# Tokens transposed by a matmul with a diagonal of 1/rms, the prompt's pieces in a bank of their own, in one core's hybrid retention and RG-LRU step

## The chip, the core and the metric

The kernel runs on one core of a Trainium2 chip. Its engines work side by side, each through its own queue in program order: TensorE (PE, with its weight loads PEld), VectorE (DVE), ScalarE (ACT), GpSimd (POOL) and SyncE (SP), which here issues the DMA transfers. The metric is the device time of one execution in microseconds; a lower one is better. A measurement of three runs spreads by about 0.1%, so a difference under 0.2% counts as none.

## The reference, cut to what matters

One layer over 512 sample tokens and 128 prompt tokens of 1024 channels, all in fp32. Each group has its own shift and scale, made from a conditioning vector; the normalized and modulated tokens `h` feed one wide projection, and everything after it hangs on `h`:

```python
mod = jax.nn.silu(cond) @ w_ada + b_ada
shift, scale, gate = jnp.split(mod, 3, axis=-1)
h = rmsnorm(x, norm_w) * (1.0 + scale[:, None]) + shift[:, None]
z = h @ w_in                      # q, k, v, gates, RG-LRU inputs, merge gates
...                               # retention, RG-LRU, merge, w_out
return x + gate[:, None] * out, s_ret, s_lru
```

## The kernel before

Nearly all of the time is matmuls in three passes of fp32r parts (high x high, high x low, low x high). These are issued by `mm3` (lines 414 to 416), and the rest of the program keeps TensorE supplied. The change lies wholly in the start, before the first projection can run; there the order of each engine's work is written out by hand, and a planner (`Plan`) orders ACT and DVE only from the loop over `kt` (line 903) on. The start runs like this:

- `load_x` brings five tiles of 128 tokens (four of the sample, one of the prompt), `load_ada` and `load_wf` bring the weights of the modulation and of the first projection, all through SP's queue. Before them SP issues `pv`, a table of small vectors.
- `warm(n)` issues n matmuls of the identity with itself, 128x128 in fp32; their result is never read. It is called as `warm(8)`, then `warm(9)` after each token tile, and twice `warm(2)` between transposes. An fp32 matmul shows as two records in the trace, a transpose as one.
- `norm_x(t)`: ACT squares and sums a token tile and takes the root of the mean; DVE takes the reciprocal and scales the tile, 128x1024, in place.
- `x_T(kt)`: five transposes on TensorE, one for each token tile, bring 128 channels by 640 tokens into a PSUM tile `z` of two banks (512 sample columns in the one, 128 prompt columns in the other), and ACT or DVE copies both parts into `fulls[kt]`. There are eight `kt`, and three PSUM tiles `z` that take turns.
- `mod_mm(kt)`: eight fp32 matmuls make shift and scale of 128 channels; ACT or DVE copies them out; `mod_cols(kt)` turns them into columns by four small fp32 matmuls (lines 766 and 767), and DVE finishes `mB` and `mA`.
- `h_mod(kt)`: ACT and DVE make the modulated tokens and split them into `hTh` and `hTl`.
- `z_first(i, kt)`: six fp32r matmuls of the first projection, for three blocks i. In the loop over `kt` they alternate with `mod_mm(kt + 2)`, `mod_cols(kt + 2)`, and the splits of the weights, `wf_high` and `wf_low`.

Of the kernel before, what the change touches and what calls it, by code (L numbers as in the profile page):

```python
# [10 lines left out]
AF = mybir.ActivationFunctionType  # L11
ALU = mybir.AluOpType
MUL, ADD, SUB = ALU.mult, ALU.add, ALU.subtract
# [289 lines left out]
def tile_hybrid_step(  # L303
# [14 lines left out]
    nc = tc.nc  # L318
    S = Plan()
    act, dve, pool, pe = nc.scalar, nc.vector, nc.gpsimd, nc.tensor  # L320
    act0, dve0 = Direct(act, S, "act"), Direct(dve, S, "dve")
# [12 lines left out]
    W6, WL = Slots(S), Slots(S)  # L334
    raws.add(perm, [f"raw{i}" for i in range(4)])

    def f32(ap):
        return ap.bitcast(F32)

    def wide(name, r=False):  # L340
        return W6.take([128, NT], F32R if r else F32, name)
# [41 lines left out]


    pv = cst.tile([128, NV], F32, name="pv")
    nc.sync.dma_start(out=pv, in_=vec)
    ident = cst.tile([128, 128], F32, name="ident")
    small = cst.tile([128, 160], F32, name="small")
    sp = cst.tile([128, 28], F32, name="sp")
# [233 lines left out]
    xt = [xp.tile([128, D], F32, name=f"x{t}") for t in range(5)]  # L623
# [9 lines left out]
    def load_x(t):  # L633
        src = x_sample[128 * t:128 * t + 128, :] if t < 4 else x_prompt
        nc.sync.dma_start(out=xt[t], in_=src)

    def load_ada(kt):
        ts = []
        for c in range(4):
            t = ada.take([128, 512], F32, "adr")  # L640
            nc.sync.dma_start(out=t, in_=w_ada[kt, :, c])
            ts.append(t)
        ada_raw[kt] = ts

    def load_wf(kt):
        t = raws.take([128, 384], F32, "wfr")
        nc.sync.dma_start(out=t, in_=w_first[kt])
        wf_raw[kt] = t

    def wf_high(kt):  # L650
        wf_hl[kt] = slab.take((perm,))
        act0.activation(wf_hl[kt][0][:, 0:384], wf_raw[kt], AF.Copy)

    def wf_low(kt):
        hi, lo = wf_hl[kt]
        dve0.tensor_tensor(lo[:, 0:384], wf_raw[kt], f32(hi[:, 0:384]), op=SUB)
        raws.give(wf_raw.pop(kt))

    for t in range(5):
        load_x(t)  # L660
    for kt in range(4):
        load_ada(kt)
# [66 lines left out]
    def psz():  # L729
        return zp.tile([128, 2, 512], F32, tag="z", name="z")  # L730
# [3 lines left out]
    def warm(n):  # L734
        for _ in range(n):
            pe.matmul(out=mb[1][:, 384:512], lhsT=ident, rhs=ident, start=True, stop=True)  # L736

    warm(8)

    def norm_x(t):  # L740
        r = rst[:, t:t + 1]
        act0.activation(sq.rearrange("p a b -> p (a b)"), xt[t], AF.Square, accum_out=ssq[:, t:t + 1])
        act0.activation(r, ssq[:, t:t + 1], AF.Sqrt, scale=1.0 / D, bias=epsc)
        dve0.reciprocal(r, r)
        dve0.tensor_scalar(xt[t], xt[t], r, None, op0=MUL)

    def mod_mm(kt, eng=act0):
        b = mb[kt % 2]  # L750
        for k in range(8):
            g = slice(32 * (k % 4), 32 * (k % 4) + 32)
            w = ada_raw[kt][k // 2][:, 256 * (k % 2):256 * (k % 2) + 256]
            pe.matmul(out=b[g, 0:256], lhsT=c32[:, k], rhs=w, start=(k < 4), stop=(k > 3))
        S.pe += 1070.0
        for t in ada_raw.pop(kt):
            ada.give(t)
        if eng is act0:
            act0.activation(mod4[kt % 2], b[:, 0:256], AF.Copy)
        else:  # L760
            dve0.tensor_copy(mod4[kt % 2], b[:, 0:256])

    def mod_cols(kt):
        m, b = mod4[kt % 2], mb[kt % 2]
        sel = pv[:, V_SEL:V_SEL + 2]
        pe.matmul(out=b[:, 256:258], lhsT=m[:, 0:128], rhs=sel, start=True, stop=True)
        pe.matmul(out=b[:, 258:260], lhsT=m[:, 128:256], rhs=sel, start=True, stop=True)
        S.pe += 300.0
        dve0.tensor_scalar(mB[:, kt], b[:, 256:258], col(V_BSH, kt), None, op0=ADD)
        dve0.tensor_scalar(mA[:, kt], b[:, 258:260], bsc1[:, kt:kt + 1], col(V_NW, kt), op0=ADD, op1=MUL)  # L770

    fulls, ready = {}, {}
    groups = ((slice(0, 512), 1), (slice(512, 640), 0))

    def x_T(kt, eng=act0):
        full = wide("hf")
        fulls[kt] = full
        z = psz()
        for t in range(5):
            o = z[:, 1, 0:128] if t == 4 else z[:, 0, 128 * t:128 * t + 128]  # L780
            pe.transpose(o, xt[t][:, 128 * kt:128 * kt + 128], ident)  # L781
        for c, src in ((groups[0][0], z[:, 0]), (groups[1][0], z[:, 1, 0:128])):
            if eng is act0:
                act0.activation(full[:, c], src, AF.Copy)
            else:
                dve0.tensor_copy(full[:, c], src)

    def h_mod(kt, both=False):
        full = fulls[kt]
        for c, g in groups:  # L790
            a, b = mA[:, kt, g:g + 1], mB[:, kt, g:g + 1]
            if both:
                act0.activation(hTh[:, kt, c], full[:, c], AF.Identity, scale=a, bias=b)
        for c, g in groups:
            a, b = mA[:, kt, g:g + 1], mB[:, kt, g:g + 1]
            if both:
                dve0.tensor_scalar(full[:, c], full[:, c], a, b, op0=MUL, op1=ADD)
            else:
                act0.activation(full[:, c], full[:, c], AF.Identity, scale=a, bias=b)
        if not both:  # L800
            act0.activation(hTh[:, kt], full, AF.Copy)
        dve0.tensor_tensor(hTl[:, kt], full, f32(hTh[:, kt]), op=SUB)
        ready[kt] = S.clock["dve"]
# [58 lines left out]

    for t in range(5):
        norm_x(t)
        warm(9)
    x_T(0)
    x_T(1, dve0)
    wf_high(0)
    wf_low(0)
    warm(2)  # L870
    mod_mm(0, dve0)
    load_ada(4)
    load_wf(4)
    x_T(2)
    warm(2)
    mod_cols(0)
    x_T(3, dve0)
    x_T(4)
    h_mod(0, True)
    x_T(5)  # L880
    mod_mm(1)
    x_T(6)
    wf_high(1)
    wf_low(1)
    x_T(7)
    xtp.__exit__(None, None, None)
    ttp, tr = open_pool("ttp", "right")
    tts.add(tr, [f"tt{i}" for i in range(3)])
# [406 lines left out]
    qk, v, o, pt, kd = {}, {}, {}, {}, {}  # L1295
# [696 lines left out]
```

## Time and profile before

| | |
|---|---|
| median of three runs | 999.16 us (998.46 to 999.55) |
| the profiled execution | 999.01 us |
| its span, first to last instruction | 997.2 us |
| TensorE busy | 981.6 us, 98% of the span |
| VectorE, ScalarE busy | 732.3 us, 543.6 us |
| mean granted TensorE clock | 0.997 of full speed |

The median includes what lies outside the span, about 1.8 us in the profiled execution. Busy time of TensorE counts the warming matmuls too, so it doesn't tell useful work from filler.

### The profile page before, as it was taken

Reading aid. Unit: us, or ns where it says so; the run is one execution under the profiler, and the core shown is the slowest. Engines: PE = TensorE matmul, PEld = TensorE weight load, DVE = VectorE, ACT = ScalarE, POOL = GpSimd, SP = SyncE. Lnnn points to the kernel's source line nnn. Section 1 sums busy time; section 2 is a strip of 40 time slices with the busy share of each in tenths; the row PEclk is TensorE's granted clock in tenths of the full one; section 3 lists DMA queues with packets and bytes.
Section 4 is the critical chain, followed back from the end, with each engine's and each line's share of the span. In section 5 each row is a group of like instructions: output and inputs, shape, how many; then the busy total and the mean of one; then the engine's idle time right before and its main releaser. Section 6 shows DMA issues by size and latency. Waiting matters only on the chain.

```text
span 997.2 us, 15542 instructions
## 1 busy us (share of the span) xinstructions
PE 981.6 (98%) x6079; PEld 918.0 (92%) x6079; DVE 732.3 (73%) x1133; ACT 543.6 (55%) x856; POOL 2.2 (0%) x13
## 2 busy tenths in 40 slices
PE   9999999999999999999999999999899999999997
PEld 8889999999999999999888888888789999999886
DVE  4699977779986799783775887877768877646554
ACT  6665554486544765652468596485574535324222
POOL 0000000000000000000000000000000000000000
PEclk9999999999999999999999999999999999999999
DMA  9745444333553335344532635454627554745312
GB/s 328 247 138 171 156 142 138 127 126 131 182 172 128 111 130 178 134 138 164 190 116 101 203 116 176 136 175 153 206 93 290 191 184 165 240 124 176 118 64 84
DMA packets 62167, 158.15 MB, mean 159 GB/s; under 512 B 6906, under 2 KB 10126, under 8 KB 62094
## 3 DMA queue, kind: packets, MB, share of 16 engines
q1 hardware_dynamic: 62094, 157.16, 46.9%
q8 instruction: 47, 0.77, 0.3%
q14 instruction: 26, 0.21, 0.1%
HBM read 119.51 MB, written 37.63 MB: 158 GB/s over the span
## 4 chain that ended last, share of the span: by engine, by line
PE 91%; DVE 4%; ACT 3%; issue 1%; DMA 1%; POOL 0%; DVEq 0%; POOLq 0%; ACTq 0%
PE z L414 29%; PE z L415 29%; PE z L416 29%; PE b L736 1%; PE z L1522 1%; ACT hf L294 1%; DVE sl L420 1%; ACT hTh L294 1%; DVE hTl L294 1%; DMA y<-sg 0%; DMA yf<-y 0%; ACT sh L539 0%; PE z L781 0%; ACT gt L1181 0%; DVE st L1416 0%
## 5 line engine op out<-in xcount | busy, mean ns | idle before, releaser
L420 DVE TENSOR_TENSOR sl<-raw,sh 128x1024 fp32r<-128x1024 f32 (+1 forms) x128 | 133.2, 1045 | 50.2 <-ACT sh L505 49.8
L505 ACT ACTIVATE sh<-raw 128x1024 fp32r<-128x1024 f32 (+1 forms) x96 | 96.8, 1013 | 120.2 <-PE z L415 75.9
L414 PE MATMUL z<-sh,sh 128*128 128x320 f32 x512 | 158.5, 310 | 0.7 <-ACT p L1007 0.7
L416 PE MATMUL z<-sh,sl 128*128 128x320 f32 x512 | 158.4, 309 | 0.0
L415 PE MATMUL z<-sl,sh 128*128 128x320 f32 x512 | 158.4, 309 | 0.0
L414 PE MATMUL z<-hTh,sh 128*128 128x320 f32 x432 | 134.6, 311 | 1.1 <-ACT hTh L294 1.1
L415 PE MATMUL z<-hTl,sh 128*128 128x320 f32 x432 | 133.4, 309 | 0.7 <-DVE hTl L294 0.7
L416 PE MATMUL z<-hTh,sl 128*128 128x320 f32 x432 | 133.2, 308 | 0.0
L414 PEld LDWEIGHTS z<-sh,sh 128*128 128x128 f32 x512 | 96.1, 188 | 1.3 <-ACT p L1007 1.3
L415 PEld LDWEIGHTS z<-sl,sh 128*128 128x128 f32 x512 | 96.1, 188 | 0.0
L416 PEld LDWEIGHTS z<-sh,sl 128*128 128x128 f32 x512 | 96.1, 188 | 0.0
L414 PEld LDWEIGHTS z<-hTh,sh 128*128 128x128 f32 x432 | 81.1, 188 | 3.9 <-issue 2.5
L415 PEld LDWEIGHTS z<-hTl,sh 128*128 128x128 f32 x432 | 81.1, 188 | 1.1 <-DVE hTl L294 1.1
L416 PEld LDWEIGHTS z<-hTh,sl 128*128 128x128 f32 x432 | 81.1, 188 | 0.0
L414 PE MATMUL z<-yh,sh 128*128 128x320 f32 x256 | 79.4, 310 | 1.6 <-ACT gt L1181 1.5
L415 PE MATMUL z<-yl,sh 128*128 128x320 f32 x256 | 79.2, 309 | 1.0 <-DVE yl L420 1.0
L416 PE MATMUL z<-yh,sl 128*128 128x320 f32 x256 | 79.0, 309 | 0.0
L414 PE MATMUL z<-sh,hTh 128*128 128x512 f32 x160 | 63.7, 398 | 0.0
L415 PE MATMUL z<-sl,hTh 128*128 128x512 f32 x160 | 63.2, 395 | 0.0
L416 PE MATMUL z<-sh,hTl 128*128 128x512 f32 x160 | 63.2, 395 | 0.0
L1054 ACT ACTIVATE p<-z 128x320 f32<-128x320 f32 x32 | 14.0, 437 | 67.3 <-PE z L416 67.3
L414 PEld LDWEIGHTS z<-yh,sh 128*128 128x128 f32 x256 | 48.1, 188 | 2.2 <-ACT gt L1181 1.7
(256 smaller groups left out, 2240.3 us busy)
## 6 DMA issues: line engine op xcount, KB each, us to landing
raw<-in_w_str_dram SPq DMA_DIRECT2D x131, 512.0 KB, 3.8
adr<-in_w_ada_dram SPq DMA_DIRECT2D x32, 256.0 KB, 5.9
g<-c SPq DMA_DIRECT2D x16, 320.0 KB, 2.1
sg<-g SPq DMA_DIRECT2D x16, 320.0 KB, 4.0
y<-sg SPq DMA_DIRECT2D x16, 320.0 KB, 2.2
yf<-y SPq DMA_DIRECT2D x16, 320.0 KB, 4.6
out_dram<-kv SPq DMA_DIRECT2D x16, 256.0 KB, 2.8
x<-c SPq DMA_DIRECT2D x10, 320.0 KB, 4.0
```

The lines of the kernel that those rows point to most:

```text
L294: return f(*args, **kw)
L414: pe.matmul(out=out, lhsT=lh, rhs=rh, start=start, stop=False, **kw)
L415: pe.matmul(out=out, lhsT=lh, rhs=rl, start=False, stop=False, **kw)
L416: pe.matmul(out=out, lhsT=ll, rhs=rh, start=False, stop=stop, **kw)
L420: dve.tensor_tensor(out, full, f32(hi), op=SUB)
L505: act.activation(hi[:, 0:w], raw, AF.Copy)
L736: pe.matmul(out=mb[1][:, 384:512], lhsT=ident, rhs=ident, start=True, stop=True)
L1054: act.activation(self.tmp[:, 2], self.a[:, 0:H], AF.Copy)
L1522: pe.transpose(z[:, 128 * t:128 * t + 128] if t < 4 else zp_[:, 0:128], o[t][:, 128 * i:128 * i + 128], ident)
```

## The change

The scaling by 1/rms leaves the token tiles and enters the transposes: `norm_x` now makes a 128x128 diagonal of 1/rms for each token tile (`dg`), and `x_t` multiplies the token tile by it in a plain fp32 matmul, which transposes and scales at once. The sample pieces of two `kt` share a PSUM tile. The prompt pieces of all eight `kt` go into one PSUM tile of their own, `zpr`, and DVE copies them out one by one. The first `mod_mm(0)` stands ahead of the transposes of `kt` 2 to 7. `warm(9)` becomes `warm(15)`, and the two `warm(2)` go. `pv` is issued by ACT's queue instead of SP's.

```diff
-    nc.sync.dma_start(out=pv, in_=vec)
...
-    for t in range(5):
+    load_x(0)
+    nc.scalar.dma_start(out=pv, in_=vec)
+    for t in range(1, 5):
         load_x(t)
...
+    dg = wide("dg")
+
     def norm_x(t):
...
-        dve0.tensor_scalar(xt[t], xt[t], r, None, op0=MUL)
+        dve0.tensor_scalar(dg[:, 128 * t:128 * t + 128], ident, r, None, op0=MUL)
...
-    def x_T(kt, eng=act0):
...
+    def x_t(o, kt, t):
+        pe.matmul(out=o, lhsT=xt[t][:, 128 * kt:128 * kt + 128], rhs=dg[:, 128 * t:128 * t + 128], start=True, stop=True)
+
+    def x_s(kt, z):
+        for t in range(4):
+            x_t(z[:, kt % 2, 128 * t:128 * t + 128], kt, t)
+
+    def ev_s(kt, z, eng=act0):
+        if eng is act0:
+            act0.activation(fulls[kt][:, 0:512], z[:, kt % 2], AF.Copy)
+        else:
+            dve0.tensor_copy(fulls[kt][:, 0:512], z[:, kt % 2])
+
+    def ev_p(kt):
+        dve0.tensor_copy(fulls[kt][:, 512:640], zpr[:, kt // 4, 128 * (kt % 4):128 * (kt % 4) + 128])
...
     for t in range(5):
         norm_x(t)
-        warm(9)
-    x_T(0)
-    x_T(1, dve0)
-    wf_high(0)
-    wf_low(0)
-    warm(2)
+        warm(15)
+    for kt in range(8):
+        fulls[kt] = wide("hf")
+    z01 = psz()
+    x_s(0, z01)
+    x_s(1, z01)
+    ev_s(0, z01)
+    ev_s(1, z01, dve0)
+    zpr = psz()
+    for kt in range(8):
+        x_t(zpr[:, kt // 4, 128 * (kt % 4):128 * (kt % 4) + 128], kt, 4)
+    for kt in range(8):
+        ev_p(kt)
     mod_mm(0, dve0)
     load_ada(4)
+    z23 = psz()
+    x_s(2, z23)
+    x_s(3, z23)
+    ev_s(2, z23)
+    wf_high(0)
+    ev_s(3, z23, dve0)
+    wf_low(0)
     load_wf(4)
-    x_T(2)
-    warm(2)
     mod_cols(0)
-    x_T(3, dve0)
-    x_T(4)
+    z45 = psz()
+    x_s(4, z45)
+    x_s(5, z45)
+    ev_s(4, z45)
     h_mod(0, True)
-    x_T(5)
     mod_mm(1)
-    x_T(6)
+    z67 = psz()
+    x_s(6, z67)
+    x_s(7, z67)
+    ev_s(5, z45, dve0)
+    ev_s(6, z67)
+    ev_s(7, z67, dve0)
     wf_high(1)
     wf_low(1)
-    x_T(7)
```

TensorE's queue at its beginning, before the change (`b<-ident` is a warming matmul, `z<-ident,x` a transpose of a token tile):

```order
L736 MATMUL b<-ident 128x128 x53
L781 MATMUL z<-ident,x_107 128x128
L781 MATMUL z<-ident,x_108 128x128
L781 MATMUL z<-ident,x_109 128x128
L781 MATMUL z<-ident,x_110 128x128
L781 MATMUL z<-ident,x_111 128x128
```

The same place after it (`z<-dg,x` is a matmul of a token tile with the diagonal):

```order
L737 MATMUL b<-ident 128x128 x83
L780 MATMUL z<-dg,x_106 128x128
L780 MATMUL z<-dg,x_107 128x128
L780 MATMUL z<-dg,x_108 128x128
L780 MATMUL z<-dg,x_109 128x128
```

The queue has 30 warming matmuls more ahead of the first token tile, and the prompt's tile x_110 no longer stands among the first.

VectorE's queue from its last scaling, before the change (`hf<-z` copies transposed tokens out of PSUM, `mod` holds shift and scale):

```order
L294 TENSOR_SCALAR x_111<-x_111,rst 128x1024
L294 COPY hf<-z 128x512
L294 COPY hf<-z 128x128
L294 TENSOR_TENSOR sl<-wfr,sh 128x384
L294 COPY mod_115<-b 128x256
L294 TENSOR_SCALAR mB<-b,pv 128x2
```

The same stretch of VectorE's queue after it:

```order
L294 TENSOR_SCALAR dg<-ident,rst 128x128
L294 COPY hf<-z 128x512
L294 COPY hf<-z 128x128 x8
L294 COPY mod_114<-b 128x256
L294 COPY hf<-z 128x512
L294 TENSOR_TENSOR sl<-wfr,sh 128x384
L294 TENSOR_SCALAR mB<-b,pv 128x2
```

Eight prompt copies now stand in one block ahead of the copy of `mod`, and another 512-column copy stands ahead of `mB`. From the loop over `kt` on, every queue has the same rows as before.

## Rows read from the trace of the kernel before

**Rows 1.** The page: span, busy time, and the chain that ended last, by engine.

```profile
span 997.2 us, 15542 instructions
...
PE 981.6 (98%) x6079; PEld 918.0 (92%) x6079; DVE 732.3 (73%) x1133; ACT 543.6 (55%) x856; POOL 2.2 (0%) x13
...
PE 91%; DVE 4%; ACT 3%; issue 1%; DMA 1%; POOL 0%; DVEq 0%; POOLq 0%; ACTq 0%
```

**Rows 2.** Chain of waits, 0 to 24 us: start us, length us, what.

```profile
1.36 13.99 PE b L736 x106
15.35 1.09 PE z L781 x10
16.44 0.45 PE b L736 x4
16.88 1.00 PE b L754 x16
17.89 0.70 PE z L781 x5
...
19.37 1.17 PE z L781 x10
```

**Rows 3.** Timeline of PE, two short windows: start, length, instruction, records merged.

```profile
3.65 1.70 PE L736 MATMUL b<-ident 128*128 128x128 f32 x7
...
8.82 0.94 PE L736 MATMUL b<-ident 128*128 128x128 f32 x7
```

**Rows 4.** Timeline of all engines, 0 to 13 us: loads and norms of the tokens.

```profile
0.74 0.39 SPq L386 DMA_DIRECT2D pv<-in_vec_dram  x1
...
5.51 1.03 ACT L294 ACTIVATE z<-x 128x1024 f32<-128x1024 f32 x1 [0.53 <-DMA x<-in_x_sample_dram]
...
12.69 0.75 DVE L294 TENSOR_SCALAR x<-x,rst 128x1024 f32<-128x1024 f32 x1
```

**Rows 5.** Timeline, 21 to 30 us: the first modulated tokens and the loop's beginning.

```profile
21.21 1.20 ACT L294 ACTIVATE hTh<-hf,mB,mA 128x512 fp32r<-128x512 f32 x2
...
23.11 0.41 PE L414 MATMUL z<-hTh,sh 128*128 128x320 f32 x1
23.77 0.42 PE L415 MATMUL z<-hTl,sh 128*128 128x320 f32 x1 [0.25 <-DVE hTl L294]
...
25.04 1.07 PE L754 MATMUL b<-adr,c 128*32 128x256 f32 x16
...
27.11 0.38 PE L766 MATMUL b<-pv,mod 128*128 128x2 f32 x2
...
27.58 0.39 PE L414 MATMUL z<-hTh,sh 128*128 128x320 f32 x1
...
28.55 0.31 PE L414 MATMUL z<-hTh,sh 128*128 128x320 f32 x1
```

**Rows 6.** Timeline of PE, 29 to 55 us: two of five `mod_mm`, and `kt` 7.

```profile
29.52 1.07 PE L754 MATMUL b<-adr,c 128*32 128x256 f32 x16
...
46.70 1.07 PE L754 MATMUL b<-adr,c 128*32 128x256 f32 x16
...
53.95 0.41 PE L414 MATMUL z<-hTh,sh 128*128 128x320 f32 x1 [1.11 <-ACT hTh L294]
```

**Rows 7.** Waits of PE, 20 us to the end: total us, times, longest us.

```profile
PE z L414 <- ACT pph L1419: 2.9, 1, 2.9
PE z L414 <- ACT gt L1181: 1.5, 1, 1.5
PE z L414 <- ACT hTh L294: 1.1, 1, 1.1
```

**Rows 8.** Groups of DVE by shape, 0 to 24 us: busy us, mean ns, idle before.

```profile
L294 DVE COPY hf<-z 128x512 f32<-128x512 f32 x2 | 1.4, 692 | 3.2 <-PE z L781 3.2
...
L294 DVE COPY hf<-z 128x128 f32<-128x128 f32 x2 | 0.6, 280 | 0.0
```

**Rows 9.** Busy time by stretch: PE, PEld, DVE, ACT, POOL, granted clock, DMA share, GB/s.

```profile
15.00:20.00 5.00, 5.00 (x54) 4.30 (x53) 2.19 (x6) 1.94 (x5) 0.00 (x0) 1.00 1.06 396
```

More of the change, by code (lines that the diff above doesn't have):

```diff
@@ L773, in tile_hybrid_step @@
     groups = ((slice(0, 512), 1), (slice(512, 640), 0))
-    def x_T(kt, eng=act0):
[L776 to L786, printed above, removed]
+    def x_t(o, kt, t):
[10 more added lines that the diff above has]
+        dve0.tensor_copy(fulls[kt][:, 512:640], zpr[:, kt // 4, 128 * (kt % 4):128 * (kt % 4) + 128])
     def h_mod(kt, both=False):
@@ L864, in tile_hybrid_step @@
         norm_x(t)
-        warm(9)
-    x_T(0)
-    x_T(1, dve0)
-    wf_high(0)
-    wf_low(0)
-    warm(2)
+        warm(15)
[11 more added lines that the diff above has]
+        ev_p(kt)
     mod_mm(0, dve0)
     load_ada(4)
+    z23 = psz()
[5 more added lines that the diff above has]
+    wf_low(0)
     load_wf(4)
-    x_T(2)
-    warm(2)
     mod_cols(0)
-    x_T(3, dve0)
-    x_T(4)
+    z45 = psz()
+    x_s(4, z45)
+    x_s(5, z45)
+    ev_s(4, z45)
     h_mod(0, True)
-    x_T(5)
     mod_mm(1)
-    x_T(6)
+    z67 = psz()
[4 more added lines that the diff above has]
+    ev_s(7, z67, dve0)
     wf_high(1)
     wf_low(1)
-    x_T(7)
+    W6.give(dg)
     xtp.__exit__(None, None, None)
```

## The prediction

> **What bounds the kernel now.** I read the page first. TensorE is busy for 98% of the span and holds 91% of the chain that ended last [rows 1], so the question for any edit in the start is whether it moves the moment from which TensorE can run the projection, and whether anything later takes that back. Then I read the chain of waits over the first 24 us. It is TensorE almost without a break: 53 warming matmuls (106 records) from 1.36 to 15.35 us, then transposes, `mod_mm` and a few more warming matmuls up to 20.5 us [rows 2]. The reader should see that the warming matmuls are no harmless filler here. They sit in the same queue as the transposes, and the first transpose starts the moment they run out. The timeline says that the tokens didn't hold it up: the last scaling of a token tile starts at 12.69 us and takes 0.75 us, so it is done at 13.44 us [rows 4], 1.9 us before. So TensorE's queue, not the norms, sets the start, with only the modulation chain (ACT, then DVE) breaking in at 23 us, where the second matmul of the projection stands still for `hTl` [rows 5].
>
> After that the loop over `kt` is paced by TensorE as well: the five `mod_mm` from 29.52 to 46.70 us are 17.18 us apart in four steps, 4.30 us each [rows 6]. The waits of PE from 20 us to the end come in six groups with 7.9 us together, the largest of them 2.9 us, and in every one it waits for ACT or DVE and never for a DMA [rows 7]. Those engines get their work from the loop, and the stream of later weights is let in by buffers that the loop sets free. So a later start of the loop shifts all of it, and nothing later is bound to the clock on the wall.
>
> **The change part by part.**
>
> *Warming matmuls ahead of the first transpose.* The queue has 83 instead of 53. Seven records at full pace take 0.94 us, of which the last has about 0.28 us by itself, so one record comes every (0.94 - 0.28) / 6 = 0.111 us, and a matmul of two records takes 0.222 us. The first ones come slower, at about (1.70 - 0.5) / 6 = 0.2 us a record [rows 3]; they are the same ones in both kernels. The 30 added ones follow at full pace, so they cost 30 x 0.222 = **+6.7 us**, and the first token matmul starts at 15.35 + 6.7 = 22.0 us. The check from the other end: 166 records at 0.111 us from 1.36 us on, and 2 us for the slow ones, gives 21.8 us. Nothing else fills this: the diagonals would be ready by about 12.9 us, since the scaling shrinks from 128x1024 to 128x128 [rows 4]. The 0.6 us that DVE saves there per tile, and any gain from the tokens' loads going first in SP's queue, lie under this stretch and give nothing.
>
> *The transposes as matmuls.* Forty transposes took 0.109 us each (ten in 1.09 us) [rows 2]. Forty fp32 matmuls of 128x128 by 128x128 are what the warming matmuls are in type and shape, so I price one at 0.222 us. The bounds are 0.109 us, if they ran like transposes, and 0.222 us; I take the upper one, because operation, type and shape are those of the warming rows and the trace shows no cheaper fp32 matmul of this size.
>
> The Trainium skill speaks against this edit more strongly: "TensorE: Matmul & The Clock Gate", section "Terms", has the transpose mode four times faster for fp32 than the plain way. The rows have a factor of two (0.222 against 0.109 us). By the Trainium skill's figure one token matmul would be 0.436 us, an estimate that would add another 40 x 0.214 = 8.6 us.
>
> From the first token work to the first projection matmul, TensorE took 23.11 - 15.35 = 7.76 us before [rows 2, 5]: the forty transposes, 4 warming matmuls, two `mod_mm` of 1.0 us, one `mod_cols` of about 0.4 us. It will have 40 x 0.222 = 8.9, 2 x 1.0 and 0.4, that is 11.3 us, and the 4 warming matmuls go (their 0.9 us is not in this sum). So this stretch gets longer by **+3.5 us**, and the first projection matmul moves from 23.11 to 22.0 + 11.3 = 33.3 us.
>
> *The copies and the modulation chain beside it.* These must keep up or they add to it. The eight prompt matmuls end at about 22.0 + 16 x 0.222 = 25.6 us. DVE then copies them in at most 8 x 0.28 = 2.2 us [rows 8], to 27.8 us, and copies `mod` in a time between its 128- and 512-column copies, 0.28 to 0.69 us, to 28.1 to 28.5 us. TensorE comes to `mod_cols(0)` at 25.6 + 1.0 + 8 x 0.222 = 28.4 us. So this is even, with a wait of 0.1 us at worst. Then come DVE's copy for `kt` 3, the low split of the weights and `mA`, done by about 30 us, and ACT's copy for `kt` 4 at 30.7 to 31.2 us. ACT starts `hTh` there. Before, `hTl` was done 2.5 us after `hTh` began (21.21 to 23.7 us, where the matmul that waited for it starts) [rows 5]. That makes 33.2 to 33.7 us, against 33.3 us at which TensorE arrives and 33.5 us for the first matmul that reads it. I take nothing, and keep +0.4 us for the range.
>
> *The loop's beginning.* From the first projection matmul to that of `kt` 1, the trace has 28.55 - 23.11 = 5.44 us [rows 5]. The pieces without a wait are three `z_first` of 0.9 to 1.0 us, two `mod_cols` of 0.45 us and one `mod_mm` of 1.0 us, some 4.7 us. The 0.5 us that TensorE stood for `hTl` at 23.5 goes, since the tokens are ready by then; the 0.2 us that it waits for `mod` ahead of 27.11 us stays. So I take 4.9 us, **-0.5 us**. This part alone is a gain.
>
> *The rest.* `pv` moves from SP's queue, where its issue took 0.39 us, to ACT's [rows 4]. ACT waited 0.53 us for the first tokens at 5.51 us, so this is worth between -0.4 and +0.4 us at the norms, both under the warming stretch: 0. Weights for later `kt` are let in by `mod_mm(0)` and the first `wf_low`, which move with the rest; `mod_mm(4)` still follows 16 us after the buffers it needs come free. At `kt` 7 TensorE waits 1.11 us for `hTh` [rows 6], because ACT and DVE fall behind in the loop; they do the same work there in the same order, so I keep that wait.
>
> The sum is 6.7 + 3.5 - 0.5 = **+9.7 us** on 999.01 us of the profiled execution, 1008.7 us. That execution lies 0.15 us under the median of the runs, which changes nothing. The change in per cent is +0.97; below 0.2% (2 us) a measurement of this kernel can't tell it from none.
>
> **The rivals.**
>
> *A token matmul at the transposes' pace.* Then the second term is -0.9 us instead of +3.5, and the time 1004.2 us. For it speaks only that the product is with a diagonal; against it, that 53 products with an identity, a diagonal too, took 0.222 us each [rows 3]. Chance 0.05.
>
> *The copies hold TensorE up.* DVE now has the prompt's eight copies in one block, and ACT's and DVE's copies of one PSUM tile may follow one another instead of running side by side. If each of the four pairs costs one copy of 0.69 us more [rows 8] on the way to `hTl`, TensorE waits 2 us or a little more ahead of the loop: 1011 us. Chance 0.10.
>
> *Twice the passes per token matmul.* A product of data with a diagonal might take twice the time of the warming products, 0.44 us, since it loads new weights each time where they load the same identity: 1008.7 + 40 x 0.222 = 1017.6 us. Against it, the transposes load new tokens each time too, and keep 0.109 us [rows 2]. Chance 0.02. The factor of the Trainium skill ("TensorE: Matmul & The Clock Gate", "Terms") would come out there.
>
> *Faster: the fp32 matmuls run through at 0.111 us each.* The place is TensorE's queue from 5 to 33 us. With one record's time per matmul, the 83 would be done at 1.36 + 2 + 83 x 0.111 = 12.6 us, the token matmuls would start with the diagonals at 13 us and take 4.4 + 2.4 us, and the projection would start at 19.8 instead of 23.11 us: 995.5 us. It decides from a matmul of 0.14 us down. Against it stands the whole first row of the chain, 53 matmuls in 13.99 us [rows 2], and a granted clock of 1.00, the 2.4 GHz level, at this place, so that there is no slower level left to be freed from [rows 9]. Chance 0.02.
>
> *The delay is taken back later.* All of the waits of PE after 20 us are 7.9 us [rows 7], and most of them lie hundreds of microseconds on, behind work that shifts along. For no change, 8 us of them would have to vanish. Chance 0.02.
>
> **How the numbers follow.** The forecast holds 0.79, at 1008.7 us, and its own range is 1007.7 to 1009.7 us (the uncertain waits, and one record's rounding over 60 of them). The range for 8 in 10 reaches to the late copies above and, below, to a loop that loses its waits of 1.1 us at `kt` 7 and of 0.2 us, with a slow stretch at the beginning that is 1 us shorter than in this trace: 1006.3 to 1011.0 us. Slower by over 0.2%: forecast, the cheaper token matmul, the late copies and twice the passes, 0.96. Within 0.2%: 0.02. Faster: 0.02.
>
> **What would show it.** The warming matmuls should end at about 22 us, and the token matmuls follow them at once, with two records each and 0.22 us apart. The first fp32r matmul should stand at 33 us, the next `mod_mm` steps at 4.30 us as before, and the shift of some 9.6 us should be the same at 50 us and at the end. The forecast is wrong if the token matmuls are single records at 0.11 us, if TensorE shows waits for DVE or ACT between 22 and 33 us, or if the shift at 34 us has shrunk by the end.

## The result, and the profile after

The changed kernel takes 1009.56 us (1008.89 to 1009.81, four runs) against 999.22 us for the kernel before beside it: a ratio of 1.0104, with a 95% interval of 1.0089 to 1.0119. It is slower by 10.3 us; the forecast was 1008.7 us.

The page of the profile after, first its span and its busy time, then the chain by engine, answers to [rows 1]:

```profile
span 1008.0 us, 15722 instructions
...
PE 992.5 (98%) x6171; PEld 928.7 (92%) x6171; DVE 732.0 (73%) x1141; ACT 541.9 (54%) x848; POOL 2.2 (0%) x13
...
PE 91%; DVE 3%; ACT 3%; DMA 2%; issue 1%; POOL 0%; SPq 0%; DVEq 0%; POOLq 0%; ACTq 0%
```

TensorE's busy time grew by 10.9 us and the span by 10.8 us, and the busy share is 98% as before. A page like this can't tell a slower kernel from a better filled one, since the added filler counts as busy.

The chain of waits over the first 36 us of the kernel after, beside [rows 2] (start, length, what, records):

```profile
1.36 20.73 PE b L737 x166
22.10 3.57 PE z L780 x32
25.67 1.00 PE b L758 x16
26.67 1.98 PE z L780 x16
28.65 0.12 PE b L770 x2
28.77 0.22 PE b L771 x2
29.00 1.89 PE z L780 x16
30.89 1.00 PE b L758 x16
31.89 1.98 PE z L780 x16
```

The warming matmuls now run until 22.1 us, and the token matmuls follow at once, two records each, 0.11 us a record. The chain is TensorE alone in this whole stretch.

TensorE's timeline at the same places as [rows 5] and [rows 6]: the first projection matmul, the second, `mod_cols(2)`, the first projection matmul of `kt` 1, the first and the last of the five `mod_mm`, and `kt` 7.

```profile
33.62 0.39 PE L413 MATMUL z<-hTh,sh 128*128 128x320 f32 x1
33.97 0.42 PE L414 MATMUL z<-hTl,sh 128*128 128x320 f32 x1
...
37.57 0.38 PE L770 MATMUL b<-pv,mod 128*128 128x2 f32 x2 [0.17 <-ACT mod L294]
...
39.00 0.31 PE L413 MATMUL z<-hTh,sh 128*128 128x320 f32 x1
...
39.97 1.07 PE L758 MATMUL b<-adr,c 128*32 128x256 f32 x16
...
57.15 1.07 PE L758 MATMUL b<-adr,c 128*32 128x256 f32 x16
64.40 0.42 PE L413 MATMUL z<-hTh,sh 128*128 128x320 f32 x1 [1.12 <-ACT hTh L294]
```

From `kt` 1 on the shift stands still: 39.00 - 28.55, 39.97 - 29.52, 57.15 - 46.70 and 64.40 - 53.95 are all 10.45 us. The first and largest of the later waits of PE are the old ones too, beside [rows 7]:

```profile
PE z L413 <- ACT pph L1444: 2.8, 1, 2.8
PE z L413 <- ACT gt L1206: 1.5, 1, 1.5
PE z L413 <- ACT hTh L294: 1.1, 1, 1.1
```

### The profile page after: what moved, and what is told of

Same layout as the page of the kernel before. It is cut to its first block, busy times and chain, and to the rows that moved or that the text cites. A ratio compares the mean times of both kernels' runs of the same rounds, so it can differ in the third digit from the quotient of the medians.

```text
span 1008.0 us, 15722 instructions
## 1 busy us (share of the span) xinstructions
PE 992.5 (98%) x6171; PEld 928.7 (92%) x6171; DVE 732.0 (73%) x1141; ACT 541.9 (54%) x848; POOL 2.2 (0%) x13
## 4 chain that ended last, share of the span: by engine, by line
PE 91%; DVE 3%; ACT 3%; DMA 2%; issue 1%; POOL 0%; SPq 0%; DVEq 0%; POOLq 0%; ACTq 0%
PE z L413 29%; PE z L414 29%; PE z L415 29%; PE b L737 2%; PE z L780 1%; DMA yf<-y 1%; PE z L1547 1%; ACT hf L294 1%; DVE sl L419 1%; DMA y<-sg 1%; ACT hTh L294 0%; DVE hTl L294 0%; ACT sh L538 0%; PE b L758 0%; DVE st L1441 0%
```

## The experiments

They undo the change in parts, then vary the filler in the kernel before. Since the end of the program scatters more than the loop, each kernel has its time, from the timed runs, and its shifts, from one profiled execution. A shift is the start of an instruction of ScalarE minus the start of the same one in the trace of the kernel before, the two lists matched one by one from the last backwards, at about 42 us (in the loop), 90, 690 and 830 us; the end is the difference of the spans. The first column is the first token piece by the chain of waits (of the last two kernels by the timeline, which in the kernel before has it 0.17 us earlier than the chain). All in us; each ratio has its 95% interval. One thing has to be kept in mind for the last two shifts: the profiled execution of the kernel before has a short stretch near 722 us in which the granted clock is at its lower level (its mean from 700 to 745 us is 0.96). So have those of most other kernels, but not those of "transposes", of "order only" and of "before, 7 per tile", which gain 1.0 to 1.8 us between 690 and 830 us, where the kernel before loses.

| kernel | first token piece | shift in the loop | at 90 us | at 690 us | at 830 us | end | median, ratio (95%) |
|---|---|---|---|---|---|---|---|
| the change | 22.10 | +10.45 | +10.45 | +10.77 | +10.72 | +10.72 | 1009.56, 1.0104 (1.0089 to 1.0119) |
| 9 per tile | 15.02 | +3.37 | +4.21 | +4.49 | +6.50 | +6.49 | 1005.50, 1.0058 (1.0046 to 1.0071) |
| transposes | 23.09 | +8.29 | +8.29 | +8.28 | +7.31 | +7.31 | 1006.87, 1.0074 (1.0061 to 1.0088) |
| order only | 16.28 | +1.45 | +1.45 | +1.75 | +0.17 | +0.19 | 1000.64, 1.0011 (1.0002 to 1.0020) |
| table on SP | 21.52 | +9.87 | +10.72 | +11.03 | +10.84 | +10.83 | 1010.13, 1.0105 (1.0091 to 1.0119) |
| diagonal, 6 per tile | 12.56 | +0.92 | +0.92 | +1.24 | +1.56 | +1.58 | 1000.19, 1.0013 (1.0004 to 1.0022) |
| order, 6 per tile | 12.21 | -2.02 | -1.17 | -0.88 | +0.88 | +0.90 | 998.28, 0.9994 (0.9985 to 1.0003) |
| before, 7 per tile | 12.77 | -2.42 | -1.56 | -1.15 | -2.92 | -2.92 | 998.19, 0.9991 (0.9982 to 1.0000) |

**Fewer warming matmuls.**

```diff
-        warm(15)
+        warm(9)
```

> The changed kernel with 9 warming matmuls after each token tile instead of 15, as before the change. Queue theory: the 30 added ones cost 30 x 0.222 = 6.7 us ahead of the first token matmul (it moves from 22.1 to 15.4 us), and all of it reaches the end: 1009.6 - 6.7 = 1002.9 us. Rival (the modulation chain of ACT and DVE takes over once TensorE comes earlier): TensorE waits for it ahead of the loop and less than 5 us come back, 1005 us or more.

The first token matmul moved from 22.10 to 15.02 us (chain of waits, first two lines) and `kt` 7's first projection matmul from 64.40 to 57.31 us (timeline, last line):

```profile
1.36 13.66 PE b L737 x106
15.02 3.57 PE z L780 x32
...
57.31 0.41 PE L413 MATMUL z<-hTh,sh 128*128 128x320 f32 x1 [1.11 <-ACT hTh L294]
```

That is 7.1 us, the 6.7 us of the sum and 0.4 us of a faster beginning. So the queue theory holds for the start, and the chain of ACT and DVE did not take over. Yet the time came out at 1005.5 us, the rival's number, and for a reason that neither theory had: of the 7.1 us by which this kernel is ahead of the changed one in the loop, 2.9 us are lost again by the end (10.72 - 6.49 = 4.23 us are left). The busy time by stretch shows where (PE, granted clock, DMA share, GB/s):

```profile
50.00:55.00 5.00, 5.00 (x44) 1.00 0.35 108
55.00:60.00 5.00, 3.44 (x20) 0.93 0.33 105
60.00:65.00 5.00, 5.00 (x28) 0.73 0.47 160
65.00:70.00 5.00, 5.00 (x36) 1.00 0.36 143
720.00:725.00 5.00, 2.29 (x11) 0.99 0.75 256
725.00:730.00 5.00, 3.78 (x9) 0.50 0.27 105
730.00:735.00 5.00, 5.00 (x20) 0.83 0.80 259
```

Behind the pause at `kt` 7, and from within the pause of 3.9 us that ends at 726.22 us, the granted clock is at its lower level of 1.2 GHz for a while. This was no chance of one execution: the mean granted clock is 0.994 in all five timed runs of this kernel, against 0.997 or 0.998 in the four of the changed kernel.

**Transposes again.**

```diff
-        dve0.tensor_scalar(dg[:, 128 * t:128 * t + 128], ident, r, None, op0=MUL)
+        dve0.tensor_scalar(xt[t], xt[t], r, None, op0=MUL)
...
-        pe.matmul(out=o, lhsT=xt[t][:, 128 * kt:128 * kt + 128], rhs=dg[:, 128 * t:128 * t + 128], start=True, stop=True)
+        pe.transpose(o, xt[t][:, 128 * kt:128 * kt + 128], ident)
```

> The changed kernel, order and 15 warming matmuls kept, with the token tiles scaled in place by VectorE and transposed by transposes again. Queue theory: 40 pieces at 0.109 instead of 0.222 us, 4.4 us less, 1005.1 us. Rival (chain): the copies and splits on VectorE don't get quicker, so the second projection matmul waits for hTl until about 30.3 us where TensorE arrives at 29.3 us; 3 to 3.5 us come back, 1006.3 us.

The shift in the loop fell from 10.45 to 8.29 us while the same 83 warming matmuls ended 0.99 us later in this execution; without that it is 3.15 us, which is the rival's size and not the 4.4 us of the pieces alone. TensorE's timeline shows the two places where the rest went, `mod` and `hTl`, and the timelines of ScalarE and VectorE show why `mod` is late: one block of nine copies ahead of it, and this block begins only when ScalarE's copy out of the same PSUM tile has ended.

```profile
27.29 0.38 PE L769 MATMUL b<-pv,mod 128*128 128x2 f32 x2 [0.43 <-DVE mod L294]
...
31.91 0.41 PE L414 MATMUL z<-hTl,sh 128*128 128x320 f32 x1 [0.92 <-DVE hTl L294]
```

```profile
24.00 0.60 ACT L294 ACTIVATE hf<-z 128x512 f32<-128x512 f32 x1 [9.93 <-PE z L779]
24.62 2.27 DVE L294 COPY hf<-z 128x512 f32<-128x512 f32 x9 [9.58 <-ACT hf L294]
26.82 0.41 DVE L294 COPY mod<-b 128x256 f32<-128x256 f32 x1
```

So once TensorE needs less time for the pieces, the copies become the bound. In the changed kernel they follow one another in the same way (ScalarE's at 23.92, VectorE's at 24.55 us), and the matmuls are slow enough to hide them. Why the second copy waits for the first, no experiment here tells.

**Both undone, the order left.** The two edits above in one kernel.

> Both undone: transposes and 9 warming matmuls, so that only the order of the start is left of the change (prompt pieces apart, first modulation earlier) and the late vector table. Queue theory: 1009.6 - 6.7 - 4.4 = 998.5 us, within 0.2% of the kernel before. Rival (chain): up to 1.4 us of it are lost, 999.9 us. If the order itself costs, it stays above 1001 us.

1000.64 us, between the rival's 999.9 us and the 1001 us of an order that costs. Its 53 warming matmuls ended at 16.28 us, 0.93 us later than the 53 of the kernel before, so the order by itself makes the loop 1.45 - 0.93 = 0.5 us later (the late table is hidden here too: the last token tile is scaled at 15.25 us). Its ratio lies 0.0002 to 0.0020 above 1: hardly anything.

**The table back on SP's queue.**

```diff
     pv = cst.tile([128, NV], F32, name="pv")
+    nc.sync.dma_start(out=pv, in_=vec)
...
-    load_x(0)
-    nc.scalar.dma_start(out=pv, in_=vec)
-    for t in range(1, 5):
+    for t in range(5):
         load_x(t)
```

> The changed kernel with the table of small vectors first in SP's queue again. Queue theory: the norms come some 1.5 us earlier (first square at 5.5 instead of 7.0 us), but the warming matmuls end at 22 us either way: 1009.6 us, no change. Rival (the late table costs its 1.5 us): 1008.1 us.

The time did not move; the loop's 0.58 us less of a shift come from the warming matmuls, which ended that much earlier in this execution. ScalarE's timeline of the changed kernel shows that the step itself was not free, only hidden:

```profile
0.74 0.40 ACTq L659 DMA_DIRECT2D pv<-in_vec_dram  x1
...
4.96 0.21 ACT L294 ACTIVATE cs<-pv 128x16 f32<-128x16 f32 x1 [2.50 <-DMA pv<-in_vec_dram]
...
7.03 1.01 ACT L294 ACTIVATE z<-x 128x1024 f32<-128x1024 f32 x1
```

The first square stands at 7.03 us instead of 5.51 us [rows 4], because the table, issued at the same 0.74 us, is usable only at 4.96 us. With the table back it stands at 4.87 us. The last diagonal of the changed kernel is done at 14.48 us, 7.6 us before its warming matmuls end, so none of this reaches the loop.

**The diagonal with a short filler.** The table on SP and `warm(6)`.

> The changed kernel with the vector table first in SP's queue and 6 warming matmuls after each token tile, so that they end as the fourth diagonal is ready at about 12 us. Queue theory: the loop starts 10.0 us earlier than in the changed kernel, 0.4 us later than in the kernel before: 999.6 us, within 0.2% of it. Rival (chain or modulation weights): the loop stays 2 us or more late, 1001.2 us.

1000.19 us, the loop 0.92 us late (forecast 999.6 us and 0.4 us). So nearly the whole loss of the change can be bought back by taking out filler that hid nothing, with the norms in time: the kernel is then 0.13% behind the kernel before. But that one has more filler than it needs. Beside the next kernel, which has the same filler and the same table and differs only in how the tokens are scaled and transposed, the diagonal still costs 0.92 + 2.02 = 2.9 us at the loop and 1.9 us of the medians.

**The order with a short filler, and the kernel before with a shorter one.** The first has transposes, the table on SP and `warm(6)`; the second is the kernel before with `warm(7)`.

> Order of the change alone (transposes, tokens scaled in place), the vector table first in SP's queue again, and 6 warming matmuls after each token tile: 38 in all, which should end at about 12.0 us, when the fourth sample tile is scaled (12.1 us). Queue theory: the first transpose moves from 15.4 to 12.1 us, the prompt's wait for their tile until 13.4 us, and the loop starts 2.3 us earlier than in the kernel before: 996.9 us. Rival (the weights of the modulation arrive too late for an earlier start): no gain over the order alone at 9 warming matmuls, 999 us or more.

> The kernel before with 7 instead of 9 warming matmuls after each token tile, 10 fewer. Queue theory: they end at 13.1 instead of 15.35 us, the last token tile is scaled at 13.4 us, so 1.9 us are won at the loop: 997.3 us. Rival (the warming matmuls of the kernel before were no bound, the modulation chain was): 999.2 us.

Both win 2.0 to 2.4 us at the loop, about as forecast, the first in spite of a wait of 0.45 us for the prompt's tile. Their times miss the forecasts by 1.4 and 0.9 us: the medians are only 0.6 to 0.7 us better than the kernel before, and neither is clear of no change. In both profiles the clock was at half behind `kt` 7, and 0.85 us of the shift was gone by 90 us.

**Filler in the pauses.** Three kernels: the one with 9 per tile and the kernel before with 7 per tile, each with five warming matmuls ahead of `kt` 7; and the latter with twelve more in the pause near 720 us.

```diff
     for kt in range(8):
+        if kt == 7:
+            warm(5)
         z_first(0, kt)
...
         hook(h, "kv")
+        if h == NH - 1:
+            spare = bank()
+            for _ in range(12):
+                pe.matmul(out=spare[:, 0:128], lhsT=ident, rhs=ident, start=True, stop=True)
+            banks.give(spare)
         attend(h)
```

> The changed kernel with 9 warming matmuls per tile, and five more (1.1 us) ahead of the projection matmuls of kt 7, where TensorE otherwise pauses for 1.1 us and the granted clock was seen at half for a while behind the pause. If the pause takes the clock down, the clock stays whole there, the step of 0.8 us between 60 and 76 us goes, and the time is 1005.5 - 0.8 + 0.2 = 1004.9 us or less. If the clock falls for another reason, the step stays: 1005.7 us.

> The kernel before with 7 warming matmuls per tile (2.4 us earlier at the loop) and five more in the pause at kt 7. If it is the clock's step behind that pause (0.8 us where it came) that ate part of the earlier start, the loop's -2.3 us hold until the stage at 700 us and the time is 997.0 us. If the pause has nothing to do with it, 998.2 us as with 7 warming matmuls alone.

> The same, and 12 more warming matmuls (2.7 us) in the pause of 2.9 us ahead of the last head's attention, behind which the granted clock was at half in most of the profiled executions. If the pauses take the clock down, no stretch at half clock is left but at both ends of the span, and 1.7 us come back in the executions that had one: 996.0 us. Rival (the filler only delays the work behind it, the clock falls anyway): 997.5 to 998.5 us.

The times are 1004.33 us (ratio 1.0054, 1.0041 to 1.0066), 997.46 us (0.9982, 0.9973 to 0.9991) and 996.16 us (0.9969, 0.9957 to 0.9981). By the medians each step is better than the kernel without that filler, by 1.2, 0.7 and 1.3 us, and the last kernel is faster than both kernels of this study. The intervals of the ratios overlap from step to step, and the first two steps compare runs beside different groups of the kernel before, whose medians differ by 0.35 and 0.5 us; so a single step is less sure than the last kernel's gain. The mean granted clock of the timed runs goes the same way: 0.994 in all five of the kernel with 9 per tile, 0.997 or 0.998 in all five with the filler at `kt` 7; 0.995 to 0.997 with 7 per tile, 0.996 or 0.997 with the filler at `kt` 7, 0.998 or 0.999 with both. The stretch around `kt` 7, with 7 per tile, without and with the five matmuls:

```profile
50.00:75.00 25.00, 23.45 (x148) 0.93 0.46 158
```

```profile
50.00:75.00 25.00, 24.13 (x164) 1.00 0.49 162
```

In the three profiles with this filler the shift at 90 us is that of the loop, within 0.01 us. And the stretch around the second pause, without and with the twelve matmuls:

```profile
715.00:720.00 5.00, 2.01 (x6) 0.81 0.73 274
720.00:725.00 5.00, 5.00 (x20) 0.85 0.51 133
```

```profile
715.00:720.00 5.00, 4.55 (x33) 1.00 0.71 245
720.00:725.00 5.00, 5.00 (x22) 1.00 0.40 154
```

The wait for `pph` fell from 3.0 to 0.4 us, the matmul behind it came no more than 0.3 us later than the shift ahead of it would have it, and the clock stayed at 2.4 GHz. Since three of twelve profiles without this filler show no fall there either, the one with it is weak evidence by itself; the clock of the five timed runs is the better one.

**No warming at all.** The kernel before without `warm(8)` and `warm(9)`.

> The kernel before without the warming matmuls ahead of the first transpose (the four between the transposes stay). If they only hold up the queue, the transposes start at 13.4 us, 1.9 us earlier: 997.3 us. If they carry the clock's slow beginning, the first transposes and modulation matmuls run at half pace and give the 2 us back: 999.3 us or more.

1000.61 us, a ratio of 1.0009 (1.0000 to 1.0018). The filler is not dead weight: without it the kernel is, if anything, slower, although its queue is free. The profiled execution took 997.51 us, the shortest of twelve, so it shows only that the loop can start 1.36 us earlier without filler (21.75 instead of 23.11 us), not where the others lose. That they lose it to the clock is likely: the six runs over 1000.6 us have a mean granted clock of 0.993 to 0.995, against 0.995 to 0.999 in the 22 runs of the kernel before beside them. In which stretch it fell, no trace shows.

## Why the prediction was right, step by step

*The filler ahead of the first transpose, +6.7 us:* right. It measured 22.10 - 15.35 = 6.75 us, and taking it out moved the loop by 7.1 us. The ground for it was one row, the chain's first: the transposes began when the warming matmuls ran out and not when the tokens were scaled.

*The transposes as matmuls, +3.5 us:* right, and a little small. From the first token matmul to the first projection matmul it takes 33.62 - 22.10 = 11.52 us instead of 7.76 us, **+3.8 us**. The matmuls have two records each at the warming matmuls' pace, so the warming rows priced them and the transposes' row did not. The Trainium skill's factor of four between the two ways ("TensorE: Matmul & The Clock Gate", "Terms") is not what this kernel shows: it is two (0.222 against 0.109 us).

*The copies beside it, 0:* right for the changed kernel, within 0.1 us: the second projection matmul comes 0.35 us after the first, where it comes 0.25 us after it in an `mm3` without a wait. It is no general truth, since with transposes the same copies cost TensorE 0.43 + 0.92 us in two waits.

*The loop's beginning, -0.5 us:* this is the term that was mis-sized. It measured 39.00 - 33.62 = 5.38 us instead of 5.44 us, **-0.1 us**. The stand for `hTl` did get shorter (from the first projection matmul to `mod_cols(1)` it is 34.81 - 33.62 = 1.19 us, before 24.61 - 23.11 = 1.50 us). But the wait for `mod` that I kept at 0.2 us grew by nearly as much: from `z_first(1, 0)` to `mod_cols(2)` it is 37.57 - 36.24 = 1.33 us, before 27.11 - 26.04 = 1.07 us. VectorE and ScalarE of the changed kernel show the path:

```profile
33.83 1.40 DVE L294 COPY hf<-z 128x512 f32<-128x512 f32 x2
...
36.05 1.20 ACT L294 ACTIVATE hTh<-hf,mB,mA 128x512 fp32r<-128x512 f32 x2 [1.13 <-DVE mA L294]
37.16 0.36 ACT L294 ACTIVATE mod<-b 128x256 f32<-128x256 f32 x1
```

Two 512-column copies now stand on VectorE ahead of `mA(1)`; `hTh` waits for that, and the copy of `mod` stands behind `hTh` in ScalarE's queue. I had followed the copies to `hTl` for `kt` 0 and not to the next link.

*The rest, 0:* right for the time and wrong in what it said of the norms. The table was given between -0.4 and +0.4 us there; its move made the first square 7.03 - 5.51 = 1.5 us later, and the diagonals were ready at 14.5 us and not at 12.9 us. That this cost nothing is the doing of the long filler, not of the reading: with warming matmuls that end at 12.56 us, as in the diagonal with the short filler, it would by these times have stood in the way, which no run tests. (VectorE saves 0.75 - 0.29 = 0.46 us a tile, not 0.6 us.)

*The sum:* 6.75 + 3.76 - 0.06 = 10.45 us at the loop, against 9.7; the remaining 0.75 us lie in the two terms above, and some 0.3 us more came later in the profiled execution.

*Nothing is taken back or lost later:* right for this pair of kernels, and only half of the truth. The shift was constant from `kt` 1 to 90 us, and the one fall of the clock near 720 us is in both profiles, so it cancels. But with 9 warming matmuls per tile the queue alone foretold 1002.9 us and the time was 2.6 us longer, by falls of the clock at two later pauses. The prediction had no term for them, and that the changed kernel met no more of them than the kernel before was luck. For the slow beginning it allowed 1 us less than in this trace and nothing more; the same 53 warming matmuls ended between 15.02 and 16.28 us, 0.3 us earlier to 0.9 us later than the 15.35 us it read.

Of the rivals, the cheap matmul, the dearer one and the taking back are refuted by the rows above. The late copies are real, one after the other as that rival had them, and hidden. That 83 fp32 matmuls run through in half the time is refuted by the 20.73 us of the chain's first row (by its own figures that rival's time is 999.0 - 3.3 = 995.7 us, not 995.5 us).

## What to carry to other kernels

Filler shares its queue with the work that it warms the engine for: compare where the filler ends with where its successor's inputs are ready, and size it by that difference (here not to nothing: without any, the kernel was no faster). An engine's busy share doesn't show this; the chain of waits does. Price a changed operation by the row that has its type and shape, even if that row is filler, and follow a block of copies to every consumer behind it, not only to the first one.

## What the runs showed of the hardware that was not expected

The granted clock fell to its lower level at short pauses of TensorE. Behind the pause at `kt` 7 (1.1 and 0.4 us of waits) it did so in 4 of 10 profiled executions without filler there, and in none of 3 with it. Near 720 us (2.7 to 3.9 us of waits) it did so, within the pause or up to 1.5 us behind it, in 9 of 12 without filler and not in the one with it. Over 25 us one such dip shows as a mean granted clock of 0.93, so 0.07 x 25 = 1.75 us of TensorE's full pace, of which 0.85 us reached the path at `kt` 7. The filler's effect fits the medians and the mean granted clock of the timed runs too, but three profiles don't prove it for `kt` 7; and why some kernels and executions dip and others don't, or twice as long near 720 us, stays open.

The beginning scatters as well. In both of these stretches by twos, from the kernel with 9 per tile and from the one with the order only, TensorE does nothing but the same warming matmuls, and the view states a clock of 1.00:

```profile
4.00:6.00 2.00, 2.00 (x17) 1.00 1.04 417
6.00:8.00 2.00, 2.00 (x20) 1.00 1.02 420
```

```profile
4.00:6.00 2.00, 2.00 (x12) 1.00 1.03 416
6.00:8.00 2.00, 2.00 (x14) 1.00 1.03 422
```

The records per stretch (17 and 20 against 12 and 14) show that the full pace came later in the second; its 53 matmuls ended 16.28 - 15.02 = 1.26 us later, which at half pace is some 2.5 us more of the slow beginning. The column of the clock does not show this.
